# Second and third modulation of a hybrid diffusion layer: summed over tiles of inputs by ScalarE and GpSimd

## The chip, the core and the metric
The kernel runs on one core of one Trainium2 chip. Its time is device microseconds of one execution; a kernel's time is the median of several runs. A profile is of one execution, with that execution's own time beside it.

## What is computed
One layer of a diffusion backbone: 512 latent tokens and 256 context tokens, 1024 channels, all in float32.

```
cond = silu(c)                                     # one vector of 1024 inputs
mod  = (cond @ w_mod + b_mod).reshape(6, 1024)     # w_mod is 1024 x 6144
h = rmsnorm(x) * (1 + mod[1]) + mod[0]             # first sub-layer: conv, gated recurrence, attention
x = x + mod[2] * merge(conv(h), recurrence(h), attention(h))
h = rmsnorm(x) * (1 + mod[4]) + mod[3]             # second sub-layer: mixture of experts
x = x + mod[5] * experts(h)
```

The six rows of `mod` are made in three groups of 2048 outputs. The first group (rows 0 and 1, for tokens and context) is needed at once. The second (rows 2 and 3) and the third (rows 4 and 5) are needed only behind the merge of the branches. The change is about those two.

## The kernel before
The program is one stream of steps, written in an order that a function sets by hand: `weave(fg, bg)` puts a list of background steps among a list of foreground steps, in proportion to the costs of the foreground. Each engine runs its own instructions in the order in which the steps were written, and waits where an operand is not there yet. SyncE (SP) issues every DMA in the same order.

*First stage.* x, the first group of w_mod (8 MB) and the first items of the input projection `w_in` are loaded. Then item after item of `w_in` (256 columns each) is multiplied with the normed input in three passes (`proj` and `value_steps`; L453 and L542 are their products on TensorE). `split_item` makes the two parts of a float32 weight that these passes need: ScalarE copies a quarter of an item (L366, a cast), VectorE subtracts (L367). A load of item n+2 is issued when use of item n begins.

*Second and third modulation.* `load_slab` (L481) loads 128 inputs x 2048 outputs as four tiles of 128x512 from two pools; `mod_step` multiplies them by `cs`, a 128x32 tile whose first two columns hold silu of the two condition vectors: `mod_mm` (L316) has four products, one for each block of 512 outputs, into four blocks of 32 partitions of one bank, accumulated over eight steps of 128 inputs. That is 16 steps for the two groups. `mod_rows` (L320) adds the bias, `mod_end` (L326, L328) transposes rows into columns. The steps are background of the second half of the value projection and of the first head's gates, ahead of the recurrence.

*Recurrence.* For each of four heads `head_proj` projects the gates of both directions (`ev_f`, L625 to L640: ScalarE takes the sigmoid, VectorE four scalings L627 to L630, then GpSimd a chain of 15 small products, L638 and L640, for the context keys) and the queries and read-out gate. `head_steps` does the head before: `diag` (L683), then seven levels. `update(l)` (L709 to L711, on VectorE) multiplies keys, queries and gate products in place; before it ScalarE copies what it will overwrite (`copies`, L695, L696). `level(l)` is four products on TensorE (L724) into one of two banks "hg", which VectorE merges with `copy_predicated` (L725). Level l's products can begin only when the copy of level l-2 has read its bank. States and outputs follow. The projections of head h are the foreground of the steps of head h-1, so there are four such stretches: heads 1, 2, 3, and the attention's queries behind the last. Here they are called the first to the fourth window.

Then come attention, merge, output projection, router and experts; the expert weights (403 MB) are streamed at over 420 GB/s while they are used.

Of the kernel before, what the change touches and what calls it, by code (L numbers as in the profile page):

```python
# [10 lines left out]
F32 = mybir.dt.float32  # L11
# [3 lines left out]
AF = mybir.ActivationFunctionType  # L15
ALU = mybir.AluOpType
# [6 lines left out]
KT = D // 128  # L23
# [123 lines left out]
def mixer_moe(ctx: ExitStack, tc: tile.TileContext, a, out):  # L147
# [10 lines left out]
    def bank(tag):  # L158
        return psum.tile([128, 512], F32, tag=tag, name=tag, bufs=pbufs[tag])
# [42 lines left out]
    cc = small([128, KT, 2], "cc")  # L202
# [11 lines left out]
    def bias_row(g):  # L214
        t = g512()
        SP.dma_start(out=t, in_=bass.AP(tensor=a["b_mod"].tensor, offset=a["b_mod"].offset + g * 2048,
                                        ap=[[512, 4], [0, 32], [1, 512]]))
        return t
# [21 lines left out]
    V.memset(cs, 0.0)  # L240
    csg = small([128, KT, 2], "csg")
    S.activation(csg, cc, AF.Sigmoid)
    V.tensor_tensor(cs[:, :, 0:2], cc, csg, op=ALU.mult)

    def rsqrt_newton(v, sd, r, b):
        S.activation(sd, v, AF.Sqrt)
# [67 lines left out]
    def mod_mm(pm, k, wm):  # L314
        for j in range(4):
            PE.matmul(pm[32 * j:32 * j + 32], cs[:, k], wm[j], start=(k == 0), stop=(k == KT - 1))  # L316

    def mod_rows(pm, brow, keep=False):
        mr = small([128, 512], "mod_r") if keep else g512()
        V.tensor_tensor(mr, pm, brow, op=ALU.add)  # L320
        return mr
# [150 lines left out]


    slabs, mods = {}, {}

    def load_slab(s):
        if s < 16 and s not in slabs:
            g, k = 1 + s // KT, s % KT
            slabs[s] = [(y512 if j < 2 else g512)() for j in range(4)]
            for j in range(4):  # L480
                SP.dma_start(out=slabs[s][j], in_=a["w_mod"][k * 128:(k + 1) * 128,  # L481
                                                            g * 2048 + 512 * j:g * 2048 + 512 * j + 512])

    def mod_step(s):
        def f():
            g, k = 1 + s // KT, s % KT
            if k == 0:
                mods["b"] = bias_row(g)
                mods["p"] = bank("acc")
            for n in range(4):  # L490
                load_slab(s + n)
            mod_mm(mods["p"], k, slabs.pop(s) if k < KT else None)
            if k == KT - 1:
                mods["r", g] = mod_rows(mods["p"], mods["b"], g == 2)
        return f

    def mod_end(g):
        def f():
            mods["c", g] = mod_cols(g, mods["r", g])
        return f  # L500
# [17 lines left out]
            G.tensor_copy(mflat[:, 448 * n:448 * n + 448], mt_[:, :448])  # L518
        SP.dma_start(out=wr_sb, in_=a["w_router"].rearrange("p (k e) -> p k e", e=NE))

    mod_bg = [mod_step(s) for s in range(8)] + [mod_end(1)] + [mod_step(s) for s in range(8, 16)] + [mod_end(2), mod_5]


    hv_t = per.tile([128, 8, 512], F32, tag="acc", name="hv", bufs=1)
# [538 lines left out]
        ring[n] = t.rearrange("p (k f) -> p k f", f=w)  # L1063


    for s in range(2):
        load_slab(s)
    x0, ff, fq = head_proj(0)
    weave(fq + use_item(1, [value_steps(0)]), ctx_bg + mod_bg[:3])
    weave(use_item(2, [value_steps(1)]) + ff, [load_masks] + mod_bg[3:])  # L1070
    xs = [x0]
    rest = []

    def mix(core, ops, every=3):
        res, ops = [], list(ops)
        for i, f in enumerate(core):
            res.append(f)
            if i % every == every - 1 and ops:
                res.append(ops.pop(0))
        return res + ops  # L1080

    for h in range(1, HEADS):
        xh, ff, fq = head_proj(h)
        xs.append(xh)
        core, nrest = head_steps(h - 1, xs[h - 1])
        weave(ff + fq, mix(core, rest))
        rest = nrest
    def insert(fg, ops):

# [13 lines left out]
    fgk = []  # L1103
    for c in range(2):
        fgk += use_item(12 + c, [proj(12 + c, b, ev_k(2 * c + b), True) for b in range(2)])
    weave(insert(fgq, ops) + fgk[:6], mix(core, rest))
    fgk = fgk[6:]
    ops = [(3, 0.5, nrm_q.sums(get("q", 2), 2, 0)), (3, 0.3, nrm_q.sums(get("q", 3), 3, 0)), (1, 0.01, nrest[1]), (3, 0.3, nrest[3])]
    ops += [(p, 0.01, f) for p, f in zip((5, 7, 9, 11), nrm_q.chain())]
# [397 lines left out]
```

## Time and profile before

| | us |
|---|---|
| median of 3 runs (1719.26 to 1721.31) | 1720.46 |
| the profiled execution, its own time | 1719.64 |
| its span, first to last instruction | 1717.5 |
| TensorE busy | 1610.1 (94%) |
| VectorE, ScalarE, GpSimd busy | 569.8, 367.6, 79.7 |

The span leaves out 2.1 us around the program. Busy shares of the whole span say little here: TensorE is busy from the second fortieth of the span to the last, the DMA queues are full from the twentieth on, and VectorE's work lies in the first third. The windows of the recurrence have to be read one by one.

### The profile page before, as it was taken

The numbers are of one execution on the slowest core, as the hardware profiler recorded it, in microseconds if no ns is written. First come the engines' busy times: TensorE is split into PE (matmuls) and PEld (weight loads), VectorE is DVE, ScalarE is ACT, GpSimd is POOL, SyncE is SP. The second block draws the span as 40 slices with busy tenths as digits, with TensorE's granted clock in tenths as the row PEclk, the third lists the DMA queues.
The fourth block names the chain that finished last, engine by engine and source line by source line (L and its number), as shares of the span: only waits on it lengthen the run. The fifth ranks groups of instructions, "written<-read, shape, count | busy, mean of one in ns | idle before, by whom it ended". The sixth has DMA issues, their size and how long they took to land.

```text
span 1717.5 us, 20477 instructions
## 1 busy us (share of the span) xinstructions
PE 1610.1 (94%) x8382; PEld 903.4 (53%) x8382; DVE 569.8 (33%) x1135; ACT 367.6 (21%) x759; POOL 79.7 (5%) x150
## 2 busy tenths in 40 slices
PE   4999999999999999999999998898898998988988
PEld 2767888777777888894343342332322422423322
DVE  3517776446664333433111121121111111211211
ACT  4414445334444232231000010000000000000000
POOL 0314330000000000000000000000000000000000
PEclk8999999999999999999999999999999999999999
DMA  9870112112221242557999999999999999999997
GB/s 348 276 255 25 50 50 74 50 68 68 68 86 68 94 152 86 197 211 285 426 426 427 426 427 427 427 426 427 427 427 427 426 427 427 426 427 426 427 426 316
DMA packets 80745, 487.77 MB, mean 284 GB/s; under 512 B 8972, under 2 KB 12556, under 8 KB 25740
## 3 DMA queue, kind: packets, MB, share of 16 engines
q1 hardware_dynamic: 80652, 486.47, 69.4%
q8 instruction: 66, 1.08, 0.2%
q14 instruction: 27, 0.22, 0.0%
HBM read 484.34 MB, written 2.10 MB: 283 GB/s over the span
## 4 chain that ended last, share of the span: by engine, by line
PE 50%; DMA 37%; DVE 4%; ACT 1%; issue 0%; SPq 0%; DVEq 0%; ACTq 0%
PE pj L453 19%; DMA W<-in_w_exp_dram 11%; DMA B<-in_w_exp_dram 9%; PE pj L1372 8%; DMA A<-in_w_exp_dram 7%; DMA D<-in_w_exp_dram 5%; DMA C<-in_w_exp_dram 5%; PE pj L1023 4%; PE acc L1399 4%; PE pj L1204 3%; PE hg L1340 2%; PE hg L1429 1%; PE hg L894 1%; PE acc L941 1%; PE hg L724 1%; PE tp L924 1%
## 5 line engine op out<-in xcount | busy, mean ns | idle before, releaser
L453 PE MATMUL pj<-A,W 128*128 128x512 f32 x1536 | 408.6, 405 | 2.9 <-ACT W L366 1.9
L453 PEld LDWEIGHTS pj<-A,W 128*128 128x128 f32 x1536 | 274.8, 190 | 71.9 <-issue 21.0
L367 DVE TENSOR_TENSOR W<-W 128x512 fp32r<-128x512 f32 (+1 forms) x184 | 122.4, 688 | 148.0 <-ACT W L366 147.6
L1372 PE MATMUL pj<-W,xe 128*64 128x512 f32 x688 | 159.2, 599 | 9.1 <-DMA W<-in_w_exp_dram 8.8
L1432 DVE TENSOR_TENSOR acc<-acc,hg 128x512 f32<-128x512 f32 x120 | 77.1, 683 | 219.2 <-PE hg L1429 219.2
L1379 ACT ACTIVATE s<-pj 128x512 f32<-128x512 f32 x32 | 19.1, 597 | 513.1 <-PE pj L1372 513.1
L1372 PE MATMUL pj<-A,xe 128*64 128x512 f32 x512 | 118.7, 600 | 6.8 <-DMA A<-in_w_exp_dram 6.8
L1372 PEld LDWEIGHTS pj<-W,xe 128*64 128x64 f32 x688 | 45.6, 136 | 114.5 <-issue 82.9
L1372 PE MATMUL pj<-B,xe 128*64 128x512 f32 x432 | 101.3, 599 | 4.0 <-DMA B<-in_w_exp_dram 3.9
L366 ACT CAST W<-W 128x512 fp32r<-128x512 f32 (+1 forms) x184 | 103.1, 600 | 0.0
L1381 DVE TENSOR_TENSOR s<-s,pj 128x512 f32<-128x512 f32 x32 | 21.9, 684 | 232.5 <-PE pj L1372 232.5
L1420 DVE TENSOR_TENSOR ye<-mod,acc 64x512 f32<-64x512 f32 x30 | 20.6, 686 | 186.8 <-PE acc L1399 186.3
L1399 PE MATMUL acc<-W,at 128*64 128x512 f32 x320 | 74.0, 600 | 8.6 <-DMA W<-in_w_exp_dram 8.6
L1372 PEld LDWEIGHTS pj<-A,xe 128*64 128x64 f32 x512 | 33.5, 136 | 83.9 <-issue 61.8
L1389 ACT COPY at<-tp 128x512 f32<-128x512 f32 x32 | 18.8, 586 | 255.9 <-PE tp L1387 255.3
L1429 PE MATMUL hg<-ye,oht 64*128 64x512 f32 x240 | 67.7, 641 | 0.0
L1372 PEld LDWEIGHTS pj<-B,xe 128*64 128x64 f32 x432 | 28.5, 136 | 69.6 <-issue 54.7
L1399 PE MATMUL acc<-B,at 128*64 128x512 f32 x240 | 56.6, 600 | 8.6 <-DMA B<-in_w_exp_dram 8.6
L453 PEld LDWEIGHTS pj<-C,W 128*128 128x128 f32 x384 | 59.1, 190 | 9.1 <-ACT y L625 0.8
L1372 PE MATMUL pj<-C,xe 128*64 128x512 f32 x256 | 59.0, 597 | 4.1 <-DMA C<-in_w_exp_dram 4.1
L453 PE MATMUL pj<-C,W 128*128 128x256 f32 x384 | 61.6, 283 | 0.0
L1340 PEld LDWEIGHTS hg<-ot,xn 128*128 128x128 f32 x512 | 58.5, 193 | 2.7 <-issue 2.7
(287 smaller groups left out, 1772.7 us busy)
## 6 DMA issues: line engine op xcount, KB each, us to landing
W<-in_w_exp_dram SPq DMA_DIRECT2D x126, 1024.0 KB, 19.5
A<-in_w_exp_dram SPq DMA_DIRECT2D x88, 1024.0 KB, 19.6
B<-in_w_exp_dram SPq DMA_DIRECT2D x85, 1024.0 KB, 19.5
C<-in_w_exp_dram SPq DMA_DIRECT2D x42, 1024.0 KB, 19.6
D<-in_w_exp_dram SPq DMA_DIRECT2D x42, 1024.0 KB, 19.6
W<-in_w_in_dram SPq DMA_DIRECT2D x34, 1024.0 KB, 4.8
y<-in_w_mod_dram SPq DMA_DIRECT2D x32, 256.0 KB, 5.6
g<-in_w_mod_dram SPq DMA_DIRECT2D x32, 256.0 KB, 5.0
```

What stands on the lines that cost most here:

```text
L366: S.copy(hi[:, sl], raws[n][:, sl])
L367: V.tensor_tensor(lo[:, sl], raws[n][:, sl], hi[:, sl].bitcast(F32), op=ALU.subtract)
L453: PE.matmul(dst, w[wi][:, k, 128 * b:128 * b + 128], src[xi][:, k], start=(k == 0 and p == 0), stop=(k == KT - 1 and p == 2))
L1023: PE.matmul(st["p"], wb[wi][:, 4 * br + k], yv[br][k][xi], start=(k == 0 and p == 0), stop=(k == 3 and p == 2))
L1204: PE.matmul(st["p"][:, 256 * u:256 * u + 256], mm[k][mi][:, ts], w[wi][:, k], start=(k == 0 and p == 0), stop=(k == KT - 1 and p == 2))
L1340: PE.matmul(px[:, 128 * k:128 * k + 128], xn[:, i, 128 * kk:128 * kk + 128], ot[:, 128 * i:128 * i + 128], start=(i == 0), stop=(i == 3))
L1372: PE.matmul(pg[64 * u:64 * u + 64], xp[:, kk, 64 * (e % 2):64 * (e % 2) + 64], wt[:, k, 512 * u:512 * u + 512], start=(kk == 0), stop=(kk ...
L1381: V.tensor_tensor(est["s", j], est["s", j], pg, op=ALU.mult)
L1399: PE.matmul(est["y"][64 * u:64 * u + 64], lhs, wt[:, k, 512 * u:512 * u + 512], start=(kk == 0), stop=(kk == 15))
L1420: V.tensor_tensor(ye[us], mod5[us, 512 * u:512 * u + 512], y[us], op=ALU.mult)
L1429: PE.matmul(pc, oht[64 * u:64 * u + 64, 128 * i:128 * i + 128], ye[64 * u:64 * u + 64], start=True, stop=True)
L1432: V.tensor_tensor(av, av, pc, op=ALU.add)
```

## The change
Each of the 64 tiles of 128 inputs x 512 outputs (8 blocks of inputs, 4 of outputs, 2 groups) is now a step of its own. ScalarE multiplies the tile by the condition's value of each input, in place (L496, a scale for each partition); for the first block of inputs it writes into one of four accumulators instead. GpSimd adds the tile to its accumulator (L498): 56 additions of 128x512. When a group's 32 tiles are done, `mod_sum` (L505) sums over the 128 partitions: one product with ones for each of the four blocks. The loads keep their bytes; they go through four buffers of an attention pool, issued three steps ahead. Four steps stand at the end of the first value projection, ten in the stage where the 16 steps stood, 14 entries in each of the first three windows (`among` puts them between the steps of the recurrence) and the other 15 in the fourth. The two transposes (`mod_end`) go to the fourth window too.

```diff
@@ -240,7 +240,8 @@
     V.memset(cs, 0.0)
     csg = small([128, KT, 2], "csg")
     S.activation(csg, cc, AF.Sigmoid)
-    V.tensor_tensor(cs[:, :, 0:2], cc, csg, op=ALU.mult)
+    V.tensor_tensor(csg, cc, csg, op=ALU.mult)
+    V.tensor_copy(cs[:, :, 0:2], csg)
 
     def rsqrt_newton(v, sd, r, b):
         S.activation(sd, v, AF.Sqrt)
@@ -472,26 +473,37 @@
 
 
     slabs, mods = {}, {}
+    MODS = 64
 
     def load_slab(s):
-        if s < 16 and s not in slabs:
-            g, k = 1 + s // KT, s % KT
-            slabs[s] = [(y512 if j < 2 else g512)() for j in range(4)]
-            for j in range(4):
-                SP.dma_start(out=slabs[s][j], in_=a["w_mod"][k * 128:(k + 1) * 128,
-                                                            g * 2048 + 512 * j:g * 2048 + 512 * j + 512])
+        if s < MODS and s not in slabs:
+            g, k, j = 1 + s // 32, s % 32 // 4, s % 4
+            slabs[s] = gen.tile([128, 2, 256], F32, tag="bias", name="slab", bufs=4).rearrange("p u k -> p (u k)")
+            SP.dma_start(out=slabs[s], in_=a["w_mod"][k * 128:(k + 1) * 128,
+                                                      g * 2048 + 512 * j:g * 2048 + 512 * j + 512])
 
     def mod_step(s):
         def f():
-            g, k = 1 + s // KT, s % KT
-            if k == 0:
-                mods["b"] = bias_row(g)
-                mods["p"] = bank("acc")
+            k, j = s % 32 // 4, s % 4
+            if s == 0:
+                sums = gen.tile([128, 2, 512], F32, tag="nvc", name="sums", bufs=1)
+                mods["s"] = [hv_t[:, 6], hv_t[:, 7], sums[:, 0], sums[:, 1]]
             for n in range(4):
                 load_slab(s + n)
-            mod_mm(mods["p"], k, slabs.pop(s) if k < KT else None)
-            if k == KT - 1:
-                mods["r", g] = mod_rows(mods["p"], mods["b"], g == 2)
+            if s % 32 == 24:
+                mods["b"] = bias_row(1 + s // 32)
+            acc_, w = mods["s"][j], slabs[s]
+            S.activation(w if k else acc_, w, AF.Copy, scale=csg[:, k, 0:1])
+            if k:
+                G.tensor_tensor(acc_, acc_, w, op=ALU.add)
+        return f
+
+    def mod_sum(g):
+        def f():
+            pm_ = bank("acc")
+            for j in range(4):
+                PE.matmul(pm_[32 * j:32 * j + 32], ones[:, 0:32], mods["s"][j], start=True, stop=True)
+            mods["r", g] = mod_rows(pm_, mods["b"], g == 2)
         return f
 
     def mod_end(g):
@@ -518,7 +530,18 @@
             G.tensor_copy(mflat[:, 448 * n:448 * n + 448], mt_[:, :448])
         SP.dma_start(out=wr_sb, in_=a["w_router"].rearrange("p (k e) -> p k e", e=NE))
 
-    mod_bg = [mod_step(s) for s in range(8)] + [mod_end(1)] + [mod_step(s) for s in range(8, 16)] + [mod_end(2), mod_5]
+    mod_bg = [mod_step(s) for s in range(32)] + [None, mod_sum(1)] + [mod_step(s) for s in range(32, 64)]
+    mod_bg += [None, mod_sum(2), mod_end(1), mod_end(2), mod_5]
+
+    def among(ops, more):
+
+        res, n = [], 0
+        for i, f in enumerate(ops):
+            res.append(f)
+            while n < len(more) and (n + 1) * len(ops) <= (i + 1) * len(more):
+                res.append(more[n])
+                n += 1
+        return res + more[n:]
 
 
     hv_t = per.tile([128, 8, 512], F32, tag="acc", name="hv", bufs=1)
@@ -1063,11 +1086,9 @@
         ring[n] = t.rearrange("p (k f) -> p k f", f=w)
 
 
-    for s in range(2):
-        load_slab(s)
     x0, ff, fq = head_proj(0)
-    weave(fq + use_item(1, [value_steps(0)]), ctx_bg + mod_bg[:3])
-    weave(use_item(2, [value_steps(1)]) + ff, [load_masks] + mod_bg[3:])
+    weave(fq + use_item(1, [value_steps(0)]), ctx_bg + mod_bg[:4])
+    weave(use_item(2, [value_steps(1)]) + ff, [load_masks] + mod_bg[4:14])
     xs = [x0]
     rest = []
 
@@ -1083,7 +1104,7 @@
         xh, ff, fq = head_proj(h)
         xs.append(xh)
         core, nrest = head_steps(h - 1, xs[h - 1])
-        weave(ff + fq, mix(core, rest))
+        weave(ff + fq, among(mix(core, rest), mod_bg[14 * h:14 * h + 14]))
         rest = nrest
     def insert(fg, ops):
 
@@ -1103,7 +1124,7 @@
     fgk = []
     for c in range(2):
         fgk += use_item(12 + c, [proj(12 + c, b, ev_k(2 * c + b), True) for b in range(2)])
-    weave(insert(fgq, ops) + fgk[:6], mix(core, rest))
+    weave(insert(fgq, ops) + fgk[:6], among(mix(core, rest), mod_bg[56:]))
     fgk = fgk[6:]
     ops = [(3, 0.5, nrm_q.sums(get("q", 2), 2, 0)), (3, 0.3, nrm_q.sums(get("q", 3), 3, 0)), (1, 0.01, nrest[1]), (3, 0.3, nrest[3])]
     ops += [(p, 0.01, f) for p, f in zip((5, 7, 9, 11), nrm_q.chain())]
```

**How instructions move.** TensorE, from the value projections on (L542 before and L565 now are its products, L316 a modulation step). Before:

```order
L542 MATMUL pj<-W,A 128x256 x60
L542 MATMUL pj<-W,C 128x256 x30
L316 MATMUL acc<-y,g 32x512 x2
L316 MATMUL acc<-g 32x512 x2
L542 MATMUL pj<-W,C 128x256 x12
L316 MATMUL acc<-y,g 32x512 x2
L316 MATMUL acc<-g 32x512 x2
L542 MATMUL pj<-W,C 128x256 x6
L316 MATMUL acc<-y,g 32x512 x2
L316 MATMUL acc<-g 32x512 x2
L542 MATMUL pj<-W,A 128x256 x36
```

Now:

```order
L565 MATMUL pj<-W,A 128x256 x66
L565 MATMUL pj<-W,C 128x256 x48
L565 MATMUL pj<-W,A 128x256 x96
L565 MATMUL pj<-W,C 128x256 x48
L454 MATMUL pj<-A,W 128x512 x9
L454 MATMUL pj<-C,W 128x256 x3
L454 MATMUL pj<-A,W 128x512 x3
```

No modulation product is left in this stage. Next, ScalarE in the second window, from the copies for level 2 to the next gate's sigmoid (L695, L696 before are L718, L719 now; L366 and L367 are the quarter of a weight; L625 and L648 the sigmoid of the next head's gate; L496 the new scaling). Before:

```order
L695 COPY g<-y 128x64x4
L696 COPY g<-g 128x64x4
L695 COPY g<-y 128x64x4
L696 COPY g<-g 128x64x4
L366 CAST W<-W 128x512
L695 COPY g<-y 128x32x8
L696 COPY g<-g 128x32x8
L695 COPY g<-y 128x32x8
L696 COPY g<-g 128x32x8
L625 ACTIVATE y<-pj 128x512
L626 ACTIVATE g<-pj 128x256
```

Now:

```order
L718 COPY g<-y 128x64x4
L719 COPY g<-g 128x64x4
L718 COPY g<-y 128x64x4
L719 COPY g<-g 128x64x4
L496 ACTIVATE slab<-slab,csg 128x512 x2
L367 CAST W<-W 128x512
L718 COPY g<-y 128x32x8
L719 COPY g<-g 128x32x8
L718 COPY g<-y 128x32x8
L719 COPY g<-g 128x32x8
L496 ACTIVATE slab<-slab,csg 128x512
L648 ACTIVATE y<-pj 128x512
```

Two scalings stand ahead of the quarter's cast, and a third ahead of the next gate's sigmoid. VectorE there, from the last scaling of a gate to the copy of level 2 (L725 before, L748 now; L367 before, L368 now is the subtraction behind the cast). Before:

```order
L630 TENSOR_SCALAR g<-g,olb,lb 128x256
L800 SCALAR_TENSOR_TENSOR y<-g,vecs 128x512
L367 TENSOR_TENSOR W<-W 128x512
L709 TENSOR_TENSOR y<-y,g 128x32x8
L710 TENSOR_TENSOR g<-g 128x32x8
L711 TENSOR_TENSOR g<-g 128x32
L709 TENSOR_TENSOR y<-y,g 128x32x8
L710 TENSOR_TENSOR g<-g 128x32x8
L711 TENSOR_TENSOR g<-g 128x32
L725 COPY_PREDICATED g<-masks,hg 128x512
```

Now:

```order
L653 TENSOR_SCALAR g<-g,olb,lb 128x256
L823 SCALAR_TENSOR_TENSOR y<-g,vecs 128x512
L732 TENSOR_TENSOR y<-y,g 128x32x8
L733 TENSOR_TENSOR g<-g 128x32x8
L734 TENSOR_TENSOR g<-g 128x32
L732 TENSOR_TENSOR y<-y,g 128x32x8
L733 TENSOR_TENSOR g<-g 128x32x8
L734 TENSOR_TENSOR g<-g 128x32
L368 TENSOR_TENSOR W<-W 128x512
L748 COPY_PREDICATED g<-masks,hg 128x512
```

The subtraction stood ahead of the update of level 3 and stands behind it, in front of the copy of level 2. Last, GpSimd in the second window (L661 and L663 are the chain of the gates, L498 the new additions). Before, the end of one chain is followed by the next:

```order
L638 TENSOR_TENSOR g<-g 128x4x32
L640 TENSOR_TENSOR g<-g 128x4
L638 TENSOR_TENSOR g<-g 128x2x64
L640 TENSOR_TENSOR g<-g 128x2
L638 TENSOR_TENSOR g<-g 128x128 x2
L640 TENSOR_TENSOR g<-g 128x128
```

Now:

```order
L663 TENSOR_TENSOR g<-g 128x2
L661 TENSOR_TENSOR g<-g 128x128
L498 TENSOR_TENSOR hv<-hv,slab 128x512
L498 TENSOR_TENSOR sums<-sums,slab 128x512 x2
L498 TENSOR_TENSOR hv<-hv,slab 128x512 x2
L498 TENSOR_TENSOR sums<-sums,slab 128x512 x2
L498 TENSOR_TENSOR hv<-hv,slab 128x512 x2
L498 TENSOR_TENSOR sums<-sums,slab 128x512
L661 TENSOR_TENSOR g<-g 128x128
L663 TENSOR_TENSOR g<-g 128x128
```

Ten additions stand between two chains here. A chain's last product shares a row with the next chain's first in the listing before.

## Rows read from the trace of the kernel before

**Rows 1.** Page, parts 1 and 2: span, one engine's share, TensorE's and DMA's fortieths.
```profile
span 1717.5 us, 20477 instructions
...
PE   4999999999999999999999998898898998988988
...
DMA  9870112112221242557999999999999999999997
```

**Rows 2.** Busy time by stretch: PE, PEld, DVE, ACT, POOL, granted clock, DMA.
```profile
76.00:130.00 54.00, 54.00 (x381) 36.17 (x380) 9.09 (x15) 7.47 (x14) 7.12 (x18) 1.00 0.77 276
130.00:175.00 45.00, 41.22 (x251) 35.84 (x250) 37.30 (x86) 20.27 (x47) 21.21 (x45) 0.96 0.06 24
175.00:220.00 45.00, 43.94 (x270) 37.90 (x269) 33.96 (x80) 20.56 (x48) 13.64 (x30) 1.00 0.15 54
220.00:265.00 45.00, 44.02 (x274) 38.09 (x273) 33.56 (x79) 20.56 (x48) 13.80 (x30) 1.00 0.16 60
265.00:310.00 45.00, 45.00 (x258) 37.06 (x257) 27.23 (x70) 23.66 (x54) 0.00 (x0) 1.00 0.14 52
155.00:159.00 4.00, 4.00 (x18) 3.42 (x17) 3.70 (x11) 2.65 (x7) 1.28 (x3) 0.57 0.60 252
```

**Rows 3.** TensorE in order of time around one modulation step.
```profile
76.11 0.62 PE L316 MATMUL acc<-y,g 128*32 128x512 f32 x2
...
77.11 1.69 PE L542 MATMUL pj<-W,C 128*128 128x256 f32 x12
```

**Rows 4.** Busy time by stretch, modulation products (L316) alone: PE, PEld.
```profile
76.00:130.00 54.00, 17.05 (x128) 2.52 (x128) 1.00 0.77 276
```

**Rows 5.** Waits of TensorE, 127 to 300 us: total, times, longest.
```profile
PE hg L724 <- DVE g L725: 4.8, 3, 3.1
```

**Rows 6.** TensorE in order of time: level 4 in the first two windows.
```profile
154.13 1.14 PE L724 MATMUL hg<-g 128*128 128x128 f32 x8 [3.13 <-DVE g L725]
155.02 1.54 PE L453 MATMUL pj<-A,W 128*128 128x512 f32 x3
...
159.11 0.95 PE L453 MATMUL pj<-A,W 128*128 128x512 f32 x3
...
200.03 1.13 PE L724 MATMUL hg<-g 128*128 128x128 f32 x8 [0.82 <-DVE g L725]
```

**Rows 7.** Groups by line and form, GpSimd, 530 to 710 us: an addition of 128x512.
```profile
L1030 POOL TENSOR_TENSOR g<-g 128x512 f32<-128x512 f32 x8 | 10.3, 1287 | 440.2 <-DVE g L1027 422.3 <-issue 17.9
```

**Rows 8.** GpSimd in order of time: 128x512 subtractions in the first stage.
```profile
40.82 1.51 POOL L403 TENSOR_TENSOR A<-g,A 128x512 fp32r<-128x512 f32 x1 [39.51 <-ACT W L366]
...
47.03 1.62 POOL L403 TENSOR_TENSOR A<-g,A 128x512 fp32r<-128x512 f32 x1 [0.89 <-DVE g L394]
```

**Rows 9.** VectorE in order of time beside them.
```profile
41.11 1.76 DVE L367 TENSOR_TENSOR W<-W 128x512 fp32r<-128x512 f32 x1
...
44.31 0.68 DVE L367 TENSOR_TENSOR W<-W 128x512 fp32r<-128x512 f32 x1
...
47.40 1.78 DVE L367 TENSOR_TENSOR W<-W 128x512 fp32r<-128x512 f32 x1
```

**Rows 10.** VectorE in order of time, first and second window.
```profile
152.46 0.90 DVE L367 TENSOR_TENSOR W<-W 128x512 fp32r<-128x512 f32 x1 [0.79 <-ACT W L366]
...
189.73 0.69 DVE L367 TENSOR_TENSOR W<-W 128x512 fp32r<-128x512 f32 x1 [0.79 <-ACT W L366]
...
195.84 1.01 DVE L367 TENSOR_TENSOR W<-W 128x512 fp32r<-128x512 f32 x1
...
199.18 0.71 DVE L725 COPY_PREDICATED g<-masks,hg 128x512 f32<-128x512 uint8 x1
```

**Rows 11.** Groups by line and form, ScalarE, 130 to 310 us: a pass over 128x512.
```profile
L366 ACT CAST W<-W 128x512 fp32r<-128x512 f32 x35 | 21.1, 621 | 0.0
```

**Rows 12.** GpSimd in order of time: first and last product of a chain of 15.
```profile
195.43 0.87 POOL L638 TENSOR_TENSOR g<-g 128x128 f32<-128x128 f32 x1 [25.37 <-DVE g L630]
...
202.48 0.53 POOL L638 TENSOR_TENSOR g<-g 128x128 f32<-128x128 f32 x1
```

**Rows 13.** Page, part 6: loads of modulation tiles, KB each, median us to landing.
```profile
g<-in_w_mod_dram SPq DMA_DIRECT2D x32, 256.0 KB, 5.0
```

## The prediction
> **What bounds the kernel now.** I read the page first. The span is 1717.5 us and TensorE is busy for 94% of it, in nine tenths of almost every slice from the third on; DMA is full only from the twentieth slice [rows 1]. So what happens ahead of the expert stage moves the end one for one, if it reaches TensorE: the expert loads begin when earlier work gives their buffers free, and come as much earlier or later.
>
> Then the stretches one by one [rows 2]. In the stage with the modulation products, 76 to 130 us, TensorE is busy 54.00 of 54.00 us, while VectorE, ScalarE and GpSimd have 9.09, 7.47 and 7.12 us to do. In the first three windows of the recurrence TensorE is busy 41.22, 43.94 and 44.02 of 45 us, and VectorE 37.30, 33.96 and 33.56. So work is moved from a stage in which TensorE alone is the limit into stretches in which VectorE has little left.
>
> Third, the waits. From 127 to 300 us TensorE waits for VectorE's copy of an earlier level three times, 4.8 us in all [rows 5]. In order of time these are level 4 of each window: 3.13 us in the first, 0.82 in the second [rows 6], and the rest of the 4.8 in the third. The reader is to see that VectorE has no slack just there: whatever holds it ahead of the copy of level 2, which frees the bank, is TensorE's loss.
>
> **What goes.** One modulation step takes TensorE from 76.11 to 77.11 us, 1.00 us [rows 3]; all 128 records of such products are busy for 17.05 us [rows 4], 1.07 for each of 16 steps, with the overlap of pipelined ends in it. I take 16 x 1.00 = 16.0 us. TensorE never pauses in this stage, so nothing hides them and all 16.0 come off. The ten scalings and additions that come into the stage are cheap there: 10 x 0.62 and 10 x 1.29 us (below) on two engines idle for over 46 of 54 us. The 38 us that are left hold eleven background entries, 3.5 us apart, so loads issued three steps ahead have some 10 us to land, against 5.0 for a tile now [rows 13].
>
> **What comes on TensorE.** Two sums over partitions, four products each in the form of a modulation step: 2 x 1.00 = +2.0 us. The two transposes only change place. Net on TensorE: -14.0 us.
>
> **What comes on ScalarE and GpSimd.** ScalarE gets 64 passes over 128x512, 0.62 us each by its cast of that size [rows 11], 40 us; GpSimd 56 additions, 1.29 us each by the same operation in the merge [rows 7], 72 us. Neither sum is on the path by itself: a window gets at most 14 of each, 8.7 us of ScalarE's 24 idle and 18.0 us of GpSimd's 23.8 or more [rows 2]. The fourth window gets ten additions, TensorE waits for nothing in it and GpSimd is free, so I charge it nothing but the wait of its sum.
>
> **What an addition does to VectorE.** Four GpSimd passes of 128x512 run in the first stage. Beside two of them [rows 8] VectorE's subtraction of 128x512 takes 1.76 and 1.78 us, against 0.68 when it starts beside none [rows 9]. The first ends 0.54 us after GpSimd's pass: it stood still until that was nearly done. So an addition met by dense VectorE work costs VectorE 1.08 us. Below, an addition in a gap costs nothing; above, it costs its whole 1.29. I take 1.08, since the pass measured has the same size and operands.
>
> The Trainium skill has a rule for this, in "SBUF — State Buffer", section "Who interferes with whom": a VectorE instruction with two SBUF inputs and a GpSimd instruction that reads SBUF exclude each other, and the second to start is blocked for the whole of the first. By it each of the eleven additions counted below would cost 1.29 instead of 1.08, 2.3 us more in the sum, 1726.9 us. The trace agrees up to that difference: the held subtraction lost 1.08 us, and the rows decide.
>
> **First window.** By the order, additions 11 and 12 follow the first head's first chain, which without the modulation products runs about 4 us closer to the next gate, and meet the four scalings that `diag` waits for; three more stand between the copy of level 0 and the chain ahead of level 2. 5 x 1.08 = +5.4 us. Against that, a subtraction with 0.79 us of idle time before it and 0.90 us long stood ahead of the copy of level 2 [rows 10] and now stands behind: -1.7. Together +3.7.
>
> **Second and third window.** Three additions fall between level 0 and the gate's scalings, 3 x 1.08 = 3.2; an idle time of 0.79 us [rows 10] takes part of it: 2.4. Three scalings of 0.62 stand in front of the cast and the sigmoid that VectorE waits for, 1.9 us, which overlaps with the additions; I take half, 0.9. The subtraction of 1.01 us [rows 10] now stands between the update of level 3 and the copy of level 2, and its cast only begins after the copies of level 4 and a fourth scaling: 0.62 + 0.62 on ScalarE, +1.2. Together 4.5 us, so the copy that began at 199.18 [rows 10] is that much later and level 4 waits over 5 us where it waited 0.82. A wait of 3.13 us was followed by 4 us with a granted clock of 0.57, most of it at 1.2 instead of 2.4 GHz, and three products took 1.54 us that take 0.95 soon after [rows 2, 6]; after 0.82 us nothing of the kind is seen. That is (1 - 0.57) x 4 = 1.7 us for each long wait, and it is new in these two windows. 2 x (4.5 + 1.7) = +12.4 us.
>
> **Waits of the sums.** The first sum needs addition 31, which stands on GpSimd behind a chain of 15 products that took 7.6 us, from 195.43 to 203.01 [rows 12], while TensorE reached level 4 at 200.03 [rows 6] and comes to the sum some 2 us later. Nothing overtakes a waiting product on TensorE. With a later level 4, I take 1.3 us, one addition; for the second sum, whose last tile is scaled and added a step before, half as much: +2.0 in all (bounds 0 and 6).
>
> **Sum.** -14.0 + 3.7 + 12.4 + 2.0 = +4.1 us. On the profiled execution's 1719.64 this gives 1723.7; the median of the runs stands 0.8 above it, so **1724.6 us**. About 0.2%, 3.4 us, is what a measurement of this kernel tells from no change.
>
> **Forecast and rivals**
>
> *Forecast: the windows take back more than the stage gave, 1724.6 us.* Its own range is 1719 to 1735: the second and third window without one of the two clock falls and at 3 us each, or additions at 1.29 and in twice the number. For it speaks that TensorE already waits for this VectorE copy in all three windows; against it, that VectorE is idle for 7.7, 11.0 and 11.4 us of them, mostly behind the states.
>
> *Rival 1, faster: the additions fall into those gaps.* GpSimd takes an addition when its tile is scaled, and VectorE may find it done. Then the first window's 3.7 stay, the other two cost 1 us each, without a clock fall, the sums 2.0: -14.0 + 7.7 = -6.3, 1714 us; with no cost in the windows at all, -12, 1708. It is right if the levels' waits stay under 2 us.
>
> *Rival 2, even: the windows cost 3.7 and 2 x 4.5, but the clock holds, and the sums wait little (1 us).* -14.0 + 13.7 = -0.3, 1720 us. The clock is the open point, since the trace has one wait of this length.
>
> *Rival 3, slower still: GpSimd becomes the limit.* In the first window it has 21.21 us now. Its passes beside VectorE took up to 1.62 us [rows 8]; 14 of them make 22.7, with 21.21 43.9 of 45 us. Then a buffer comes free late, SyncE waits with the tile's load and the weights behind it, and ScalarE waits in its queue for the tile, 5.0 us to landing [rows 13], with casts and copies behind. It decides when additions take over 1.7 us. One such wait in each window puts 3 x 5 us on top: 1740 us.
>
> That the products do not leave the first stage is excluded by the order: none is left there.
>
> **How the numbers follow.** Forecast 0.45, of which 0.10 lie within 0.2%; rival 1 0.30, of which 0.03 lie within; rival 2 0.16, 0.13 within, the rest split evenly; rival 3 0.09. Slower: 0.35 + 0.015 + 0.09, about 0.45; faster: 0.27 + 0.015, about 0.29; same 0.26. The range runs from 1708, rival 1 with nothing paid in the windows, to 1737, over the forecast's upper end and short of rival 3, which leaves out some 0.15.
>
> **What would show it.** Right: the stage behind the value projection is 14 to 16 us shorter with TensorE still busy throughout; TensorE waits for the copy of an earlier level over 3 us in the second and third window, with a granted clock under 0.7 behind it; VectorE's two-input operations show maxima over 1.5 us in the windows; additions take 1.3 to 1.6 us. Wrong: level 4's waits unchanged (rival 1); long waits at a clock of 1.00 (rival 2); ScalarE waiting for tiles of w_mod in the windows (rival 3); a first stage that stays longer than 42 us, which the sum has no term for.

## The result, and the profile after

The changed kernel takes 1733.89 us (median of 4 runs, 1733.47 to 1736.01) where the kernel before, on the same chip, takes 1720.8: a ratio of 1.008, 95% interval 1.0063 to 1.0098. It is 13 us slower. The forecast was 1724.6, slower, with a range to 1737: the side and the range held, but the forecast change was a third of the one that came. The profiled execution is the slowest of the four, 1736.01 us.

The stage did what the change is written for. All the modulation products of groups two and three are gone from it, and the gates of the first head come earlier by 14.0 us, in spite of a wait of 3.6 us just ahead of them. What follows gives back more than twice that. TensorE's time marks, before and after:

| mark on TensorE | before | after | difference | added in the stretch ahead |
|---|---|---|---|---|
| first product of the input projection | 39.46 | 41.36 | +1.9 | +1.9 |
| gates of head 1 (L683, now L706) | 134.31 | 120.28 | -14.0 | -15.9 |
| gates of head 2: first window | 180.92 | 168.94 | -12.0 | +2.0 |
| gates of head 3: second window | 224.79 | 224.73 | -0.1 | +11.9 |
| gates of head 4: third window | 268.62 | 275.15 | +6.5 | +6.6 |
| behind the attention's queries: fourth window | 326.80 | 344.42 | +17.6 | +11.1 |

From there on the difference stays between 16.5 and 17.6 us to the end. The first 1.9 us are not the change's: that mark lay between 39.5 and 41.4 us in the kernels of this study, and one that is the same up to there (below, the first sum without its wait) has it at 39.64.

The waits of TensorE in the changed kernel, 120 to 330 us (total, times, longest), which answer to [rows 5]:

```profile
PE acc L593 <- ACT g L848: 5.5, 1, 5.5
PE acc L505 <- POOL sums L498: 4.9, 1, 4.9
PE pj L454 <- ACT y L648: 4.7, 3, 2.6
PE hg L747 <- DVE g L748: 4.4, 2, 3.8
PE hg L706 <- DVE g L680: 3.6, 1, 3.6
PE hg L747 <- ACT W L367: 2.0, 1, 2.0
PE hg L787 <- DVE g L748: 1.1, 1, 1.1
```

Before, one pair had over 1 us, 4.8 in all; now there are seven pairs, with 26.2. The first is in the fourth window (the sums of squares of the attention's queries wait for ScalarE), the second is the first sum, ahead of level 4 of the second window; the three of L454 are products that wait for a bank that ScalarE's sigmoid empties.

Busy time by stretch in the changed kernel (PE, PEld, DVE, ACT, POOL, granted clock), around four of these waits, as in [rows 2]:

```profile
193.00:201.00 8.00, 4.88 (x17) 2.94 (x17) 6.25 (x15) 3.40 (x9) 2.91 (x6) 0.57 0.13 33
299.00:303.00 4.00, 3.58 (x11) 1.91 (x12) 3.09 (x6) 2.16 (x5) 1.27 (x1) 0.57 0.16 47
186.00:190.00 4.00, 4.00 (x19) 3.67 (x17) 3.93 (x10) 0.81 (x2) 2.31 (x4) 0.57 0.22 66
248.00:252.00 4.00, 3.57 (x15) 3.24 (x16) 4.00 (x9) 1.90 (x5) 2.75 (x5) 0.57 0.04 6
```

The reader is to see a granted clock of 0.57, most of the stretch at 1.2 GHz, around each long wait. A low clock costs time only while TensorE works. In the 8 us around the sum it stands still for the first 3, so there the stretch behind the wait is the one to read:

```profile
196.12:200.05 3.93, 3.93 (x8) 1.99 (x9) 2.93 (x9) 1.33 (x4) 0.00 (x0) 0.50 0.27 67
```

That is (1 - 0.50) x 3.93 = 2.0 us. Behind the others it is (1 - 0.57) x 4.00 = 1.7 us where TensorE is busy throughout, and 1.5 us in the two stretches of 3.6 us of work. Waits and clock together nearly make up the second window (2.6 + 1.7 + 4.9 + 2.0 + 1.0 for the sum, less the 0.8 that level 4 waited before: 11.4 against 11.9) and the third (1.7 + 3.8 + 1.5 - 0.8 = 6.2 against 6.6).

How a GpSimd addition gets to a product that has nothing to do with it shows in the fourth window. GpSimd, VectorE, ScalarE and TensorE of the changed kernel in order of time:

```profile
290.32 3.00 POOL L498 TENSOR_TENSOR hv<-hv,slab 128x512 f32<-128x512 f32 x2 [3.09 <-ACT slab L496]
295.85 1.40 POOL L498 TENSOR_TENSOR sums<-sums,slab 128x512 f32<-128x512 f32 x1 [2.53 <-ACT slab L496]
```

```profile
292.09 1.51 DVE L732 TENSOR_TENSOR y<-y,g 128x256 f32<-128x256 f32 x1
...
293.96 0.41 DVE L732 TENSOR_TENSOR y<-y,g 128x256 f32<-128x256 f32 x1
...
296.01 1.27 DVE L734 TENSOR_TENSOR g<-g 128x16 f32<-128x16 f32 x1
...
297.87 0.16 DVE L734 TENSOR_TENSOR g<-g 128x16 f32<-128x16 f32 x1
```

```profile
293.71 0.40 ACT L718 COPY g<-y 128x256 f32<-128x256 f32 x1 [2.86 <-DVE y L732]
...
297.65 0.40 ACT L718 COPY g<-y 128x256 f32<-128x256 f32 x1 [1.10 <-DVE y L732]
...
298.77 0.60 ACT L848 ACTIVATE g<-pj 128x512 f32<-128x512 f32 x1
```

```profile
292.90 1.04 PE L593 MATMUL acc<-g,consts 128*32 128x512 f32 x2
299.43 1.92 PE L593 MATMUL acc<-g,consts 128*32 128x512 f32 x2 [5.48 <-ACT g L848]
```

An update that takes 0.41 us takes 1.51 beside the additions, and one of 16 columns 1.27 where its neighbour takes 0.16. ScalarE's copies wait for these updates. The squares (L848), whose input has long been there (TensorE has done nothing since 293.9 us), stand behind the copies and a scaling in ScalarE's queue, and TensorE waits for the squares. The link that the forecast did not have is the queue of ScalarE.

### The profile page after: what moved, and what is told of

Same layout as the page of the kernel before. It is cut to its first block, busy times and chain, and to the rows that moved or that the text cites. A ratio compares the mean times of both kernels' runs of the same rounds, so it can differ in the third digit from the quotient of the medians.

```text
span 1734.1 us, 20409 instructions
## 1 busy us (share of the span) xinstructions
PE 1606.6 (93%) x8270; PEld 907.9 (52%) x8270; DVE 607.4 (35%) x1136; ACT 406.3 (23%) x823; POOL 159.7 (9%) x206
## 4 chain that ended last, share of the span: by engine, by line
PE 46%; DMA 40%; DVE 5%; ACT 2%; issue 1%; POOL 1%; SPq 0%; ACTq 0%; DVEq 0%; POOLq 0%
PE pj L454 19%; DMA W<-in_w_exp_dram 12%; DMA B<-in_w_exp_dram 10%; PE pj L1393 7%; DMA A<-in_w_exp_dram 7%; DMA C<-in_w_exp_dram 6%; DMA D<-in_w_exp_dram 5%; PE pj L1046 4%; PE acc L1420 3%; PE pj L1225 3%; PE pj L565 1%; DVE y L732 1%; PE hg L917 1%; PE acc L964 1%; PE hg L1361 1%
## 5 line engine op out<-in xcount | busy, mean ns | idle before, releaser
L454 PE MATMUL pj<-A,W 128*128 128x512 f32 x1536 | 409.4, 406 | 2.9 <-ACT W L367 1.9
L454 PEld LDWEIGHTS pj<-A,W 128*128 128x128 f32 x1536 | 276.7, 191 | 68.3 <-issue 17.7
L368 DVE TENSOR_TENSOR W<-W 128x512 fp32r<-128x512 f32 (+1 forms) x184 | 129.0, 723 | 152.8 <-ACT W L367 152.4
L367 ACT CAST W<-W 128x512 fp32r<-128x512 f32 (+1 forms) x184 | 103.4, 599 | 0.0
L454 PEld LDWEIGHTS pj<-C,W 128*128 128x128 f32 x384 | 60.2, 193 | 14.6 <-ACT y L648 6.0
L454 PE MATMUL pj<-C,W 128*128 128x256 f32 x384 | 62.5, 286 | 4.7 <-ACT y L648 4.7
```

Of the source, the lines that this page charges most:

```text
L367: S.copy(hi[:, sl], raws[n][:, sl])
L368: V.tensor_tensor(lo[:, sl], raws[n][:, sl], hi[:, sl].bitcast(F32), op=ALU.subtract)
L454: PE.matmul(dst, w[wi][:, k, 128 * b:128 * b + 128], src[xi][:, k], start=(k == 0 and p == 0), stop=(k == KT - 1 and p == 2))
```

## The experiments

Three theories. **A**: GpSimd's additions make VectorE stand still, and through it ScalarE and TensorE. **B**: it is ScalarE, with 64 more passes and with waits for tiles (rival 3's sign is there: 9.0 us in four waits, below). **C**: the windows lose by themselves, because the stage ahead is shorter and the chains have less ahead of them. The waits of ScalarE in the changed kernel, 60 to 330 us:

```profile
ACT slab L496 <- DMA slab<-in_w_mod_dram: 9.0, 4, 4.6
```

**Additions left out.**

```diff
-            if k:
-                G.tensor_tensor(acc_, acc_, w, op=ALU.add)
```

> The 56 GpSimd additions are left out (the sums hold the first tile of each column block alone); loads and the 64 scalings on ScalarE stay where they are. Theory A (the additions hold VectorE still, and the copies, sigmoids and squares behind it on ScalarE, and TensorE, come late by that): of the 27 us that the four windows give back only some 4 are left, 1708 to 1714 us, no wait of TensorE over 2 us between 120 and 320 us. Theory B (ScalarE's 64 passes of 0.72 us, and its four waits for tiles, 9.0 us in all, hold its casts and copies back): 1726 to 1734 us, with the waits of TensorE for ScalarE's sigmoid and squares still there.

1706.68 us (1705.77 to 1710.62; ratio to before 0.9925, 0.991 to 0.994), 1.3 us under the band of theory A and far from that of B. The additions are worth 27.2 us. One thing went otherwise: the third window still has one wait of 3.6 us. ScalarE still waits for tiles here, 4.9 us in four waits, and the time is good.

**Scalings left out.**

```diff
-            S.activation(w if k else acc_, w, AF.Copy, scale=csg[:, k, 0:1])
+            if k == 0:
+                S.activation(acc_, w, AF.Copy, scale=csg[:, k, 0:1])
```

> 56 of the 64 scalings on ScalarE are left out; GpSimd adds the tiles as they were loaded. Theory A (additions hold VectorE): 1726 to 1734 us, VectorE's two-input operations still with maxima over 1.5 us, the wait of the first sum of 4.9 us still there within 1 us. Theory B (ScalarE's passes and its waits for tiles): 1708 to 1716 us.

1729.73 us (1728.80 to 1731.53). Only 4.2 us come back; the first sum waits 5.9 us. The wait for the squares is down to 0.7 us, since no scaling stands ahead of them, and yet the fourth window adds 11.8 us (11.1 in the change): products of the levels wait for VectorE instead, 9.6 us in four waits against 4.4 in two. Theory B falls as the main cause, and rival 3 with it.

**Windows empty.**

```diff
-        if s < MODS and s not in slabs:
+        if s < 14 and s not in slabs:
...
+            if s >= 14:
+                return
             acc_, w = mods["s"][j], slabs[s]
```

> The first 14 steps stay in the first stage; the 50 steps of the four windows of the recurrence are left out with their loads, scalings and additions (the two sums hold the first stage's steps alone); sums, bias rows, transposes stay. Theories A and B: nothing is left that could hold the windows, 1706 to 1710 us (1720.5 - 14, and up to 4 us for the first window, in which the head's chain runs closer to its gate). Theory C (the windows lose by themselves, since the start comes 14 us earlier and the chains have less ahead of them): 1714 us or more.

1701.49 us (1700.79 to 1702.20), 4.5 us under the band: theory C falls. By the marks the first window now gives back 3.7 us, the second and third 0.3 and 0.7, and only the fourth adds, 4.2. The wait of 3.6 us at the first head's gates stays (the stage's own ten additions are still there), but the first window's wait of 3.13 us at level 4 and the clock fall behind it are gone [rows 2, 6]; the granted clock there is 1.00.

**What of an addition it is: its reads, or its place in GpSimd's queue.**

```diff
             if k:
-                G.tensor_tensor(acc_, acc_, w, op=ALU.add)
+                G.memset(w, 0.0)
+                G.memset(w, 0.0)
```

> Each of the 56 additions is replaced by two GpSimd fills of the scaled tile with zero: they stand at the same place, wait for the same scaling, hold the same buffer about as long (1.2 to 1.4 us for both), but read nothing. (The sums hold first tiles alone.) Theory A1 (the additions cost what they do because GpSimd's reads and VectorE's two-input operations shut each other out): near the kernel without additions, 1706 to 1713 us; VectorE's two-input operations show no maxima over 1 us in the windows. Theory A2 (GpSimd's own queue: its chain, the sum and the buffers stand behind the additions): 1725 to 1734 us, the wait of the first sum still there.

1710.23 us (1709.30 to 1711.04). The two fills take 0.53 and 0.55 us, so the place is held for 1.1 us instead of 1.47, a little less than was meant; yet 23.7 of the 27.2 us are gone. VectorE shows it. Its busy time (third figure) between the first and the last mark of the table above, with the same 387 instructions each time, in the kernel before, without additions, with fills, and in the change:

```profile
39.46:326.80 287.34, 277.31 (x1709) 226.23 (x1709) 174.80 (x387) 124.93 (x272) 68.53 (x135) 0.98 0.33 116
```
```profile
40.55:317.82 277.27, 263.82 (x1596) 226.44 (x1596) 174.37 (x387) 162.81 (x336) 67.15 (x135) 0.97 0.36 120
```
```profile
41.27:320.31 279.04, 264.99 (x1596) 226.19 (x1596) 175.71 (x387) 163.31 (x336) 125.99 (x247) 0.96 0.36 119
```
```profile
41.36:344.42 303.06, 272.91 (x1597) 230.83 (x1597) 212.03 (x387) 163.81 (x336) 148.52 (x191) 0.94 0.34 109
```

174.37, 175.71 and 212.03: the fills add 1.3 us to VectorE, the additions 37.7 us, 0.67 for each. One by one (ns, shortest, median and longest, 112 to 330 us), in the change the subtraction of 128x512, an update of 128x256 and the copy that reads PSUM:

```profile
L368 DVE TENSOR_TENSOR W<-W x35: 677/728/1771, 121.9 to 326.6; 128x512 fp32r<-128x512 f32 x35
```
```profile
L733 DVE TENSOR_TENSOR g<-g x48: 409/419/1523, 127.1 to 308.9; 128x256 f32<-128x256 f32 x48
```
```profile
L748 DVE COPY_PREDICATED g<-masks,hg x28: 709/731/745, 130.0 to 312.6; 128x512 f32<-128x512 uint8 x28
```

and the first two with fills:

```profile
L368 DVE TENSOR_TENSOR W<-W x39: 674/693/948, 119.6 to 326.7; 128x512 fp32r<-128x512 f32 x39
```
```profile
L734 DVE TENSOR_TENSOR g<-g x48: 405/420/742, 124.8 to 284.5; 128x256 f32<-128x256 f32 x48
```

Operations with two SBUF inputs get up to 1.1 us longer beside additions; the copy, whose inputs are a mask in SBUF and products in PSUM, does not. The Trainium skill has this in "SBUF — State Buffer", section "Who interferes with whom": a VectorE operation with two SBUF inputs contends with a GpSimd operation that reads SBUF, and not with one that only writes. These runs agree, 1771 against 948 ns.

One more thing differs in the kernel with fills: its sums read accumulators that no fill writes, so the first sum no longer waits for GpSimd at all, whatever the fills read. That wait is worth some 4 us (the kernel without it, below). Of A2, then, the place in the queue, held for 1.1 us, costs 3.5 us and the sum's wait some 4; the rest of the 27.2, near 20 us by difference, goes with the reads.

**Additions on VectorE instead.**

```diff
-                G.tensor_tensor(acc_, acc_, w, op=ALU.add)
+                V.tensor_tensor(acc_, acc_, w, op=ALU.add)
```

> The 56 additions are made by VectorE instead of GpSimd, in the same places, 0.69 us each by the subtraction of the same size. Theory A1: in the trace of the change VectorE is busy 37.6 us longer than before, 0.67 us for each addition, as much as the addition itself takes there; so the time stays within 8 us of the change, 1726 to 1738 us. Theory A2: GpSimd's chain and the buffers come free early, 1712 to 1722 us.

1720.94 us (1719.92 to 1722.23, 10 runs; ratio to before 1.0006, 0.9996 to 1.0015), inside A2's band, near its upper end, 5 us under A1's, and 13 us better than the change. The additions take 0.71 us there. A1's forecast took VectorE's total as the measure, and it is not. Between the marks VectorE is busy 209.96 us, nearly as long as in the change:

```profile
40.39:329.64 289.25, 267.18 (x1597) 225.90 (x1597) 209.96 (x443) 162.34 (x336) 73.09 (x135) 0.97 0.35 115
```

By the marks the time comes back at the gates of head 1 (18.1 us earlier than before, 14.0 in the change; the first mark is 1.0 us apart) and in the second window (3.9 us added instead of 11.9), less in the third (5.0 instead of 6.6), and not in the fourth (10.9 instead of 11.1). The first sum waits 2.1 us instead of 4.9, the gates of head 1 1.3 instead of 3.6, and sigmoids hold products for 2.8 instead of 4.7. So the additions cost 13 us more on GpSimd than on VectorE, at the same VectorE time. By the kernel with fills and the sum's wait the queue's part of that is some 7.5 us (3.5 + 4, an estimate, since the fills held their place for a shorter time). Why the same VectorE time otherwise costs less as additions than as standing still isn't settled; one difference is that an addition stands where the order puts it, while a GpSimd pass meets whichever operation comes.

**One VectorE operation for both, in the change's places.**

```diff
-            S.activation(w if k else acc_, w, AF.Copy, scale=csg[:, k, 0:1])
             if k:
-                G.tensor_tensor(acc_, acc_, w, op=ALU.add)
+                V.scalar_tensor_tensor(acc_, w, csg[:, k, 0:1], acc_, op0=ALU.mult, op1=ALU.add)
+            else:
+                S.activation(acc_, w, AF.Copy, scale=csg[:, 0, 0:1])
```

> As the change, in its places, but scaling and addition of a tile are one VectorE operation: VectorE gets 56 x some 0.75 us, no more than with plain additions on VectorE (1720.9 us), and ScalarE loses 56 passes of 0.72 us. If the passes on ScalarE were worth the 5 us that they were worth between the kernel without additions (1706.7) and the one with empty windows (1701.5): 1713 to 1718 us. If VectorE's own work is all that counts: 1719 to 1722 us.

1713.43 us (1711.42 to 1715.21; ratio 0.9961, 0.9949 to 0.9974). Without the 56 passes of ScalarE, and without VectorE's waits for them, the time is 7.5 us less than with plain additions on VectorE, and VectorE is busy as long as there:

```profile
41.41:322.06 280.65, 265.12 (x1597) 225.46 (x1597) 210.63 (x443) 128.63 (x280) 73.58 (x135) 0.97 0.36 118
```

In the change's own places the same sums are then 6.7 us faster than the kernel before, where the change is 13 slower.

**The first sum without its wait.**

```diff
-                PE.matmul(pm_[32 * j:32 * j + 32], ones[:, 0:32], mods["s"][j], start=True, stop=True)
+                PE.matmul(pm_[32 * j:32 * j + 32], ones[:, 0:32], mods["s"][min(j, g + 1)], start=True, stop=True)
```

> The first sum takes the third column block in place of the fourth (four products still, the fourth row of the second modulation is then another), so that it waits for addition 30 instead of 31, which stands behind the chain on GpSimd. If the wait of 4.9 us and the half clock behind it (6.8 us, worth 3.4) are lost time of their own: 1725 to 1728 us. If the levels behind the sum wait instead (for copies that VectorE has not made by then, as level 4 did in the forecast): under 3 us less, 1731 to 1734 us.

1729.80 us (1727.66 to 1731.01), 4.1 us less, between the bands. In this kernel's trace the sum waits for nothing, and level 4 behind it waits instead, with a granted clock of 0.61 from 192 to 196 us:

```profile
192.45 1.68 PE L747 MATMUL hg<-g 128*128 128x128 f32 x8 [2.69 <-DVE g L748]
```

So the forecast's wait of level 4 in the second window was there, behind the sum's: in TensorE's order the first sum stands ahead of level 4, not behind it.

**The fourth window's own ten steps left out.**

```diff
-        if s < MODS and s not in slabs:
+        if s < 56 and s not in slabs:
...
-                load_slab(s + n)
+                if s + n < 54:
+                    load_slab(s + n)
...
+            if s >= 54:
+                return
             acc_, w = mods["s"][j], slabs[s]
```

> The last ten steps, all that stand in the fourth window (54 to 63), are left out with their loads, scalings and additions; both sums, the bias row and the transposes stay. If the fourth window loses by its own ten steps: its share of about 9 us comes back (the wait of the sums of squares for ScalarE of 5.5 us, the clock behind it 1.7, the second sum's wait), 1722 to 1727 us. If it loses what the windows ahead of it have handed on (a late start of its chains): 1730 to 1735 us.

1729.82 us (1729.09 to 1730.14), again 4.1 us less, and 0.2 us under the second band. In its trace the fourth window adds 6.7 us (6.44 at the gates of head 4, 13.17 behind the queries) instead of 11.1; the wait for the squares is 1.9 instead of 5.5. The kernel with empty windows gives the ground to this: there the fourth window adds 4.2 us (20.8 us earlier at the gates of head 4, 16.6 behind the queries), with the second sum, the transposes and a wait for the squares of 0.9. So the 11.1 us are 4.2 that the moved work costs in any case, 2.5 that the windows ahead hand on, and 4.4 for its own ten steps: each theory has a part.

**All of it behind the attention.** The 64 steps, sums and transposes go among the gates and the merge, four steps to an item (the main lines; the sums' buffer and the load of x move as the text below says).

```diff
-    weave(fq + use_item(1, [value_steps(0)]), ctx_bg + mod_bg[:4])
+    weave(fq + use_item(1, [value_steps(0)]), ctx_bg + [None] * 4)
...
-        weave(ff + fq, among(mix(core, rest), mod_bg[14 * h:14 * h + 14]))
+        weave(ff + fq, mix(core, rest))
...
-            weave(gate_item(c), [])
+            weave(gate_item(c), mod_bg[:4])
+            mod_bg = mod_bg[4:]
...
-        weave(merge_item(dt), [])
+        weave(merge_item(dt), mod_bg[:4])
+        mod_bg = mod_bg[4:]
```

> All 64 steps, both sums and the transposes are moved out of the first stage and the recurrence into the gates and the merge behind the attention, four steps to each piece of weights, with the sums in the large buffer that is free there (x is loaded into it after the merge instead of half way). VectorE has 69 of 180 us to do there and GpSimd 9. Theories A and B: the cost hangs on how close VectorE or ScalarE is to the path, so nearly nothing is lost: 1720.5 - 16 + 2 for the sums, up to 3 for casts and subtractions that come late, and the x load: 1705 to 1711 us. Rival: additions cost VectorE wherever they stand and its subtractions of the weights come late for TensorE, 1716 to 1726 us.

1704.54 us (1702.45 to 1706.57; ratio 0.9908, 0.9894 to 0.9923), half a us under the band: 16 us under the kernel before and 29 under the change, with the same passes and additions. Busy time of this kernel while it makes the sums (PE, PEld, DVE, ACT, POOL, clock), and of the kernel before at the same place:

```profile
510.00:694.00 184.00, 184.00 (x843) 149.28 (x843) 115.06 (x115) 95.17 (x172) 91.64 (x64) 1.00 0.61 204
```
```profile
527.00:711.00 184.00, 183.64 (x839) 150.84 (x839) 70.56 (x117) 56.69 (x110) 10.30 (x8) 1.00 0.31 113
```

VectorE is busy 44.5 us longer with two instructions fewer: here too it stands still beside the additions (1.47 us each), 0.79 us for each, and the time shows none of it, since TensorE works through all 184 us. The gates of head 1 come 18.6 us earlier than before (115.73), and that holds to the merge; 3.4 us of it go back on two sums and the transposes there.

**The same with one VectorE operation.** The edit of the fused kernel above, in these places.

> As the kernel with all steps in the gates and the merge, but scaling and addition of a tile are one VectorE operation (first tiles stay on ScalarE): 56 x some 0.75 us, 42 us in a stretch of 184 us in which VectorE has 69 us to do, and neither ScalarE's pass nor GpSimd's. If TensorE, which never waited in that stretch of the kernel with GpSimd's additions, bounds it: the same time, 1702 to 1707 us. If VectorE's 23 us of standing still per 90 us there did cost something that the trace shows nowhere: under 1702 us. If longer VectorE queues delay the gates' subtractions: over 1708 us.

1704.26 us (1704.22 to 1705.65; ratio 0.9912, 0.9897 to 0.9927): the same. GpSimd and ScalarE are spared 79 and 34 us there, and none of it was on the path.

## Why the prediction had the right sign and a third of the size

What the runs give, as a ladder: 1701.5 with empty windows; +5.2 for loads and scalings (1706.7; the empty one still has the stage's ten additions, so their own cost is somewhat more); +3.5 for passes of GpSimd that only write (1710.2); +23.7 for what the additions do beyond that (1733.9), some 4 of it the first sum's wait.

- **The stage, -16.0, and 2.0 for the sums: right in kind, both too small.** With the work out of the way altogether the gates of head 1 come 18.6 us earlier, and the sums and transposes take 3.4: -15.2 net, against -14.0. The step took 16 x 1.00 from one interval; all 128 records, 17.05 us [rows 4], were the better figure.
- **First window, +3.7: near, in part by luck.** By the gates of head 2 the forecast had -16.0 + 3.7 = -12.3; the trace has -12.0, or -13.9 without the first mark's 1.9 (-13.3 and -13.4 in two kernels with the same steps up to there). The stage gave some 3 us more than the forecast had (19.4 with the first mark taken off), and the additions up to there took some 6 back instead of 3.7. The gates of head 1 wait 3.6 us for VectorE where the order had put additions 11 and 12, and level 4's old wait of 3.13 us is gone.
- **Second and third window, 6.2 us each: right in size, half right in the path.** The third adds 6.6. Level 4 waits 3.83 us in it, where over 5 were named, with the clock fall that was named; 1.7 us more come from a product that waits for ScalarE's sigmoid, which the sum has only as a delay of VectorE. The second adds 7.0 in the kernel whose sum does not wait, 6.0 without the 1.0 of the sum itself, and level 4 waits 2.69 us in it. In the change itself the sign named for the second window, a wait of level 4, is not there.
- **Waits of the sums, 1.3 us for the first: too small.** The wait for addition 31 behind GpSimd's chain was named, but level 4 was taken to wait ahead of it. TensorE comes to the sum first: 4.9 us of wait and 2.0 of clock, in place of level 4's own wait; the second window costs 11.9 - 7.0 = 4.9 us more by it. The second sum, with 0.7 in the forecast, waits for nothing.
- **The step that failed: "The fourth window gets ten additions, TensorE waits for nothing in it and GpSimd is free, so I charge it nothing but the wait of its sum."** It adds 11.1 us, where the forecast had 1.0 for the sum and 0.7 for its wait: 9.4 of the 13.5 us by which the forecast is short at the last mark of this trace (9.3 us by the medians). That TensorE waited for nothing there said that there was slack, not how much: the copies of the recurrence and the squares of the queries share ScalarE's queue. Of the 11.1, 4.4 are its own ten steps, 2.5 are handed on, and 4.2 the moved sum, transposes and their waits, of which the forecast had the sum alone, since it took the transposes as only changing place. Nor was it GpSimd that the window lacked. It adds 4.2 us with empty windows, 4.7 with scalings alone, 4.7 with fills, but 11.8 without scalings, 10.9 with the additions on VectorE and 9.0 with the fused operation: whatever takes VectorE's time costs it 9 to 12 us.
- **The price of an addition, 1.08 us, was right ([rows 9]; 1771 against 677 ns now); the count was short.** Eleven additions were counted, at the places of the first three windows where a wait was expected. VectorE loses 37.7 us over 56, as if some 35 had met it at that price. One reading behind the price was wrong: the subtraction at 44.31 us [rows 9] did not start beside none. It lies inside a GpSimd pass that the rows leave out, and that one took 2.20 us, over the 1.62 that rival 3 goes by:

```profile
43.93 2.20 POOL L403 TENSOR_TENSOR A<-g,A 128x512 fp32r<-128x512 f32 x1 [1.60 <-DVE g L394]
```

- **Scalings, 0.62 us by the row of a cast [rows 11]:** 0.72 measured, 0.10 us more over 64 passes. Additions, 1.29: 1.47 on average, 1.27 to 1.75. That the longer ones stood still for VectorE is likely, and not tested. Both small.
- **Rival 3 was not it.** Its sign, ScalarE waiting for tiles, is there, but the times without scalings (1729.7) and without additions (1706.7) decide against it.

## What to carry to other kernels

A GpSimd operation that reads SBUF is not free for a VectorE that has gaps: here each addition took 0.67 us of VectorE's time in the recurrence and 0.79 in the merge. Price it so, and ask where VectorE's lateness goes next, along every engine that waits for it in order. The total alone does not tell the time: with 210 to 212 us of VectorE's time the kernel took 1733.9, 1720.9 or 1713.4 us. Off-path work belongs in a stretch in which TensorE is busy without a pause and lateness of VectorE does not reach it; the same 56 additions cost 27 us in the recurrence, and in the merge as much as a fused operation on VectorE, with TensorE busy throughout. Where the work had to stay, one VectorE operation that scales and adds beat two passes on engines with time to spare.

## What the hardware showed that was not expected

VectorE's scaling with one SBUF input (L650, 128x512) is held as well: 479 ns at the shortest, 1117 in the median of the windows, 486 before. Beside fills it is 487 in the median and 924 at the longest. In the change:

```profile
L650 DVE TENSOR_SCALAR y<-y,nolb x7: 479/1117/1133, 115.6 to 257.1; 128x512 f32<-128x512 f32 x7
```

The forecast had counted operations with two inputs alone. The trace of the kernel before had it already, beside the GpSimd pass at 43.93 us: two such scalings take 1.97 us where the two before them take 0.99.

```profile
42.80 0.99 DVE L394 TENSOR_SCALAR g<-g,ga,modT 128x512 f32<-128x512 f32 x2
...
44.91 1.97 DVE L394 TENSOR_SCALAR g<-g,ga,modT 128x512 f32<-128x512 f32 x2
```

The same section of the Trainium skill says that an operation with one SBUF input contends only in the modes that use both ports; which mode these ran in no run here shows.
